# A two-layer encoder on one core: layer 0's V stage at 224 dense tokens instead of 240, layer 1's at 192 instead of 208, two more groups of 16 tokens by table and gather, and six dot products moved to the second half of the U stage

## The chip, the cores and the metric

The kernel runs on one core of a Trainium2 chip. The time is that of the device, in microseconds (us): the median of the runs shown. A profile is one further execution, with its own time. PE is the matrix engine, PEld its weight loads, DVE the vector engine, ACT the scalar engine, POOL the general engine (GpSimd), SP the engine that issues most DMAs here.

## The reference

272 tokens (16 learned ones and 256 of the input) of 1024 numbers go through two layers. Each has a token mixer (layer 0 a gated recurrence in both directions, layer 1 a convolution module), then an expert mixer; each of the four ends in a layer norm over a scaled residual. Nearly all the time is in the two expert mixers:

```python
q = (xc @ w_query).reshape(c, PEER_HEADS, 2, PEER_HALF)
scores = jnp.einsum('chpk,pnk->chpn', q, sub_keys.astype(q.dtype))
s1, i1 = lax.top_k(scores[:, :, 0], PEER_TOPK)
s2, i2 = lax.top_k(scores[:, :, 1], PEER_TOPK)
...
expert = idx1 * PEER_N_KEYS + idx2
g = jax.nn.softmax(s.astype(jnp.float32), axis=-1).astype(xc.dtype)
u = expert_u[expert]
act = jax.nn.gelu(jnp.einsum('chkd,cd->chk', u, xc))
v = expert_v[expert]
return jnp.einsum('chk,chkd->cd', g * act, v)
```

Each token and each of 8 heads picks 16 of 128 x 128 = 16384 experts. An expert has a row of U and a row of V, of 1024 floats each. Layer 1's output for the 16 learned tokens is dropped, so its expert mixer has 256 tokens.

## The kernel before

An expert mixer has two ways to treat a token. The **dense** way multiplies the token with all 16384 rows of U and weighs the results with a matrix that is zero but at the picked experts; then it multiplies the weighed results with all rows of V. The **few** way takes 16 tokens by 8 heads as 128 partitions and, for each of the 16 picks, gathers 128 rows (512 KB) from memory by an indirect DMA that POOL issues (`few_rows`). For U, DVE takes the dot product of the rows with the tokens (`few_mult`, from `few_dot` or from the plan); for V, DVE adds the rows with their weights into `few_out` (`few_add`), and at the end PE adds `few_out` to the accumulators with 8 products by a 0/1 matrix (L770).

A group of 16 tokens is named by its first token. The tables at the top of the file say which way each takes. Tokens below `DENSE_U[layer]` are dense in U, those below `DENSE_V[layer]` dense in V. A group in `EARLY` has its first dots during the first half of U, one in `LATE` has all its dots in the V stage. A group in `DRAWN` is dense in U but few in V: the results of its 16 tokens for all experts are written to a table in memory (`few_dump`: POOL copies a piece to the tile `own` and writes it out), and its 16 activations are then fetched with small indirect DMAs (`few_draw`, L1032; DVE first copies one column of indices to `turn`, L1031).

A layer's mixer is staged so:

- Queries and the top-k. The top-k of the second 128 tokens runs on DVE step by step beside the U stage. Its picks for the groups go through memory (`few_spread`, L994, and `few_fetch`, L998, on POOL), and DVE makes row numbers of them (`few_ids`, L1004 to L1008).
- U, first half: 64 tiles j of 128 experts. Each is one load of 512 KB by SP (`raw`, four buffers), a rounded copy on ACT (`hi`, three buffers), the rest `lo = raw - hi` (L152, two buffers), and 24 products of 128x128 by 240 tokens on PE (L180): hi by the tokens' hi and lo parts, lo by their hi part. `lo` is made by POOL up to tile 40 and by DVE from tile 41.
- U, second half: 64 tiles more, `lo` on DVE. Between them the weight matrix is made and multiplied in, for 8 dense-in-V tokens at a time (`g_unit`: 16 small products on PE, L682 and L683, and some comparisons and products on DVE). `few_dump` writes its pieces here.
- V: 128 tiles. Each is again a load, a `hi`, a `lo` on DVE, and 16 products: hi by the weighed results' hi and lo parts side by side (L732, twice the dense tokens wide) and lo by their hi part (L736, once). The split of the weighed results into parts (`w`) is made for four tiles at once. `few_plan` spreads the gathers of the few groups over tiles 2 to 112 at equal distances: step s issues gather s and then uses gather s - 2; there are three buffers `rows`. It puts the draws of a drawn group between a first tile and three tiles ahead of the group's first V row. Eight tiles before the end SP loads the saved residual `xr` (two DMAs of 512 KB, L759).

The order on each engine is made by a scheduler when the program is built; an engine runs its list in order, and an instruction that waits holds up all behind it. `issue_after(x)` ties what is traced inside it to come after x only where both are on x's engine.

Of the kernel before, what the change touches and what calls it, by code (L numbers as in the profile page):

```python
# [7 lines left out]
F32 = mybir.dt.float32  # L8
F32R = mybir.dt.float32r
F16 = mybir.dt.float16  # L10
U32 = mybir.dt.uint32
# [6 lines left out]
P = 128  # L18
# [6 lines left out]
TOPK = 16  # L25
# [8 lines left out]
FEW = META  # L34
DENSE_U, DENSE_V = (240, 240), (240, 208)
EARLY, LATE, DRAWN = ((256,), (240,)), ((240,), ()), ((), (224, 208))
DOTS_FROM, DOTS, AHEAD, LO_FROM = 48, 10, 2, 41
# [25 lines left out]
class Trunk:  # L63
# [66 lines left out]
    def load(self, src):  # L130
        raw = self.wp.tile([P, NB * P], F32, tag="raw", name="raw", bufs=4)
        parts = src if isinstance(src, tuple) else (src,)
        w = NB * P // len(parts)
        for i, part in enumerate(parts):
            self.nc.sync.dma_start(raw[:, i * w:(i + 1) * w], part)
        return raw
# [408 lines left out]
    def peer(self, layer, n, xs):  # L545
# [10 lines left out]
        with tc.tile_pool(name=f"few{layer}", bufs=1) as kp:  # L556
# [82 lines left out]
            with tc.tile_pool(name=f"act1{layer}", bufs=1) as ap1:  # L639
# [3 lines left out]
                drawn_pool = tc.tile_pool(name=f"drawn{layer}", bufs=2, side="right")  # L643
                rp = drawn_pool.__enter__()
                dumps = {}
                for g, few in enumerate(drawn):
# [47 lines left out]
                def u_out(i, ps):  # L694
# [4 lines left out]
                    if cd > 0:  # L699
                        tmp = hp.tile([P, n], F32, tag="tmp", name="tmp")  # L700
                        nc.scalar.activation(tmp[:, :cd], ps[:, :cd], AF.Gelu_apprx_tanh)
                        nc.vector.tensor_tensor(w[:, :cd], w[:, :cd], tmp[:, :cd], op=OP.mult)  # L702
                    for piece in dumps.get(i, ()):
                        few_dump(*piece)
# [5 lines left out]
                def few_dump(few, j, j1):  # L710
                    own = rp.tile([P, 32, FEW], F32, tag="own", name="own")[:, :j1 - j]
                    act, o = (act_a, 0) if j < JA else (act_b, JA)
                    nc.gpsimd.tensor_copy(own, act[:, j - o:j1 - o, few["t0"]:few["t0"] + FEW])  # L713
                    nc.gpsimd.dma_start(few["table"][:, j:j1], own)
# [33 lines left out]
                for j in range(0, NK - JG, JG):  # L748
# [5 lines left out]
                    if j == NK - 2 * JG:  # L754
                        row_pool.__exit__(None, None, None)
                        self.left_pool = tc.tile_pool(name=f"left{layer}", bufs=1, side="right")
                        xr = self.left_pool.__enter__().tile([P, NB, nq], F32, name="xr")
                        for i in range(2):
                            nc.sync.dma_start(xr[:, 4 * i:4 * i + 4, :], self.saved[:, 4 * i:4 * i + 4, :])  # L759
                    for jj in range(JG):  # L760
# [189 lines left out]
    def few_new(self, kp, layer, t0):  # L950
        few = {"t0": t0, "layer": layer, "rows": {}, "drawn": t0 in DRAWN[layer],
               "ids": kp.tile([P, 2, TOPK], U32, name=f"ids{t0}"), "act": kp.tile([P, TOPK], F32, name=f"act{t0}"),
               "z": kp.tile([P, 1, TOPK], F32, name=f"z{t0}")}
        if t0 < 2 * P:
            few["pos"] = kp.tile([P, 2, TOPK], F32, name=f"pos{t0}")
# [102 lines left out]
    def few_plan(self, vp, early, late, drawn, scale, layer, ahead=2):  # L1058
        tables = self.a["u_rows"], self.a["peer_v"].rearrange("l a b d -> (l a b) d")
        rows = [(few, i, k) for few in early + late + drawn for i in range(2)  # L1060
                for k in range((DOTS if few in early else TOPK if few["drawn"] else 0) if i == 0 else 0, TOPK)]
        begin = 2
        slots = len(rows) + ahead
        at = [begin + s * (NK - 4 * JG - begin) // slots for s in range(slots)]

        def step(s):
            if s >= ahead:
                few, i, k = rows[s - ahead]
                if i == 0:
                    self.few_mult(few, k)  # L1070
                    if k == TOPK - 1:
                        self.few_gelu(few, few is (early + late)[-1])
                else:
# [12 lines left out]
        for g, few in enumerate(drawn):  # L1086
            few["turn"] = vp.tile([P, TOPK], U32, name=f"turn{few['t0']}")
            lo, hi = begin + 14 * g, at[rows.index((few, 1, 0)) + ahead] - 3
            self.steps += [(lo + k * (hi - lo) // TOPK, lambda few=few, k=k: self.few_draw(few, k)) for k in range(TOPK)]
# [254 lines left out]
```

## Time and profile before

| | |
|---|---|
| median of 3 runs | 1810.55 us (1809.45 to 1811.69) |
| the profiled execution | 1811.96 us, span 1810.2 us |
| PE busy | 1760.8 us, 97% of the span |
| DVE busy | 1503.9 us, 83% |
| ACT busy | 908.9 us, 50% |
| POOL busy | 483.8 us, 27% |
| moved from and to memory | 396.41 MB, mean 219 GB/s |
| first half of U, layer 0 and layer 1 | about 125 to 352 and 1047 to 1269 us |
| second half of U | about 352 to 553 and 1270 to 1466 us |
| V | about 553 to 889 and 1466 to 1794 us |

The layers' expert mixers fill 125 to 889 us and 1047 to 1794 us of the span. A row of the timeline gives a start, a duration, engine and line, operation, tiles and count, and in brackets the idle time of the engine before it and what ended it. A row of the chain of waits gives start and duration of a piece of the chain that ended last. A row of the windows gives for one stretch the busy time of PE, PEld, DVE, ACT and POOL with their instruction counts, the clock that PE was granted (1.00 is full speed), the mean busy share of the DMA engines and the rate.

### The profile page before, as it was taken

To read this page: it belongs to the slowest core of one execution; us is meant where nothing else is said; L and a number is where in the kernel's file an instruction comes from. 1 tells how busy PE (TensorE), PEld (TensorE's weight loads), DVE (VectorE), ACT (ScalarE), POOL (GpSimd) and SP (SyncE) were. 2 spreads that over 40 slices of the span, in tenths; PEclk is the share of its full clock that TensorE was granted. 3 is DMA by queue.
4 is the path that set the end of the run, shared out by engine and by line. 5 is a ranking of instruction groups with operands and counts; after the bars stand their busy time and mean duration, and the time that the engine had idled before them with its cause. 6 is when DMAs were issued, how large, how long until landed. Compare 5 with 4: busy or idle time off the path is not lost.

```text
span 1810.2 us, 34904 instructions
## 1 busy us (share of the span) xinstructions
PE 1760.8 (97%) x13484; PEld 1685.9 (93%) x13484; DVE 1503.9 (83%) x2727; ACT 908.9 (50%) x1492; POOL 483.8 (27%) x328
## 2 busy tenths in 40 slices
PE   8999999999999999999998999999999999999996
PEld 7899999999999999999887899999999999999996
DVE  7786998889997777787699769998889968878875
ACT  5554444554445444885432645445454445544452
POOL 1102993100002332221000017962100035634210
PEclk9999999999999999999999999999999999999998
DMA  5446667755557888887541356578555568989973
GB/s 198 163 152 161 195 195 248 253 164 165 169 171 280 307 306 289 293 305 251 192 133 65 105 175 182 182 240 279 186 173 184 172 247 324 329 310 316 321 259 120
DMA packets 112439, 396.41 MB, mean 219 GB/s; under 512 B 13584, under 2 KB 14992, under 8 KB 112144
## 3 DMA queue, kind: packets, MB, share of 16 engines
q1 hardware_dynamic: 91632, 324.74, 53.7%
q0 software_dynamic: 20640, 69.43, 10.8%
q8 instruction: 106, 1.74, 0.4%
q14 instruction: 61, 0.50, 0.1%
HBM read 387.14 MB, written 6.98 MB: 218 GB/s over the span
## 4 chain that ended last, share of the span: by engine, by line
PE 82%; DVE 9%; DMA 3%; POOL 2%; issue 2%; ACT 1%; POOLq 0%; DVEq 0%; SPq 0%; ACTq 0%
PE u L180 40%; PE acc L732 21%; PE acc L736 12%; PE u L216 3%; DVE cy L1224 2%; POOL lo L152 2%; DVE odd L1224 2%; PE g L682 1%; PE g L683 1%; DVE lo L152 1%; DMA raw<-peer_v 1%; DMA rows<-u_rows,ids 1%; PE sps L578 1%; PE var L856 0%; PE acc L770 0%
## 5 line engine op out<-in xcount | busy, mean ns | idle before, releaser
L145 ACT ACTIVATE hi<-raw 128x1024 fp32r<-128x1024 f32 x556 | 588.6, 1059 | 625.3 <-PE u L180 190.9
L152 DVE TENSOR_TENSOR lo<-raw,hi 128x1024 fp32r<-128x1024 f32 x474 | 579.9, 1226 | 173.6 <-PE acc L736 74.7
L180 PE MATMUL u<-xs,hi 128*128 128x240 f32 (+2 forms) x4544 | 569.1, 277 | 0.6 <-DVE xs L379 0.6
L180 PEld LDWEIGHTS u<-xs,hi 128*128 128x128 f32 x4544 | 537.5, 189 | 1.5 <-DVE xs L379 1.2
L732 PE MATMUL acc<-w,hi 128*128 128x480 f32 (+1 forms) x1984 | 448.0, 368 | 4.8 <-ACT hi L145 2.9
L732 PEld LDWEIGHTS acc<-w,hi 128*128 128x128 f32 x1984 | 355.1, 189 | 29.2 <-ACT hi L145 3.2
L180 PE MATMUL u<-xs,lo 128*128 128x240 f32 (+2 forms) x2272 | 308.2, 277 | 5.4 <-POOL lo L152 3.2
L180 PEld LDWEIGHTS u<-xs,lo 128*128 128x128 f32 x2272 | 280.5, 189 | 7.5 <-POOL lo L152 4.2
L736 PEld LDWEIGHTS acc<-w,lo 128*128 128x128 f32 x2048 | 269.4, 191 | 13.5 <-DVE lo L152 5.8
L736 PE MATMUL acc<-w,lo 128*128 128x240 f32 (+1 forms) x2048 | 272.1, 274 | 4.4 <-DVE lo L152 4.4
L152 POOL TENSOR_TENSOR lo<-raw,hi 128x1024 fp32r<-128x1024 f32 x82 | 209.8, 2580 | 100.6 <-ACT hi L145 73.0
L1015 POOL DMA_INDIRECT rows<-peer_v,ids x80 | 122.3, 1529 | 237.6 <-DVE few_out L1056 171.6
L1015 POOL DMA_INDIRECT rows<-u_rows,ids x48 | 59.9, 1249 | 379.2 <-DVE act_b L702 216.0
L216 PE MATMUL u<-x,raw 128*128 128x272 f32 x480 | 114.7, 399 | 5.3 <-DMA x<-h 5.3
L216 PEld LDWEIGHTS u<-x,raw 128*128 128x128 f32 x480 | 92.9, 194 | 24.8 <-DMA raw<-w_in 5.2
L1056 DVE SCALAR_TENSOR_TENSOR few_out<-rows,act,few_out 128x1024 f32<-128x1024 f32 x75 | 96.0, 1280 | 0.0
L689 ACT ACTIVATE act_b<-g 128x432 f32<-128x432 f32 (+41 forms) x56 | 21.9, 390 | 108.8 <-DVE act_b L652 97.4
L665 DVE TENSOR_TENSOR AB<-iota,iT 128x2048 f16<-128x2048 f16 x56 | 68.1, 1219 | 0.1
L1022 DVE SCALAR_TENSOR_TENSOR rows<-rows,wide 128x1024 f32<-128x1024 f32 x48 | 58.5, 1219 | 4.2 <-DMA rows<-u_rows,ids 4.2
L682 PE MATMUL g<-AB 128*128 128x128 f16 x448 | 56.6, 220 | 0.0
L683 PE MATMUL g<-Bl,AB 128*128 128x128 f16 x448 | 56.0, 219 | 0.0
L713 POOL COPY own<-act_b 128x512 f32<-128x512 f32 (+2 forms) x6 | 5.4, 935 | 182.1 <-ACT act_b L698 182.1
(284 smaller groups left out, 1778.6 us busy)
## 6 DMA issues: line engine op xcount, KB each, us to landing
raw<-peer_u SPq DMA_DIRECT2D x256, 512.0 KB, 4.2
raw<-peer_v SPq DMA_DIRECT2D x248, 512.0 KB, 5.1
raw<-w_query SPq DMA_DIRECT2D x28, 512.0 KB, 4.0
raw<-pw SPq DMA_DIRECT2D x22, 512.0 KB, 3.5
raw<-w_in SPq DMA_DIRECT2D x16, 512.0 KB, 4.1
raw<-w_out SPq DMA_DIRECT2D x8, 512.0 KB, 3.9
raw<-peer_v SPq DMA_DIRECT2D x16, 256.0 KB, 4.5
wide<-wide SPq DMA_DIRECT2D x5, 512.0 KB, 4.3
```

What stands on the lines that cost most here:

```text
L145: self.act_hi = nc.scalar.activation(hi, raw, AF.Copy).ins
L152: i = e.tensor_tensor(lo[:, s], raw[:, s], hi[:, s].bitcast(F32), op=OP.subtract)
L180: self.mm = nc.tensor.matmul(ps[:, :n], l[:, k, :], xs(k, r)[:, :n], start=start, stop=stop)
L216: self.mm = self.nc.tensor.matmul(ps[:, :n], raw[:, k, :], x[:, k, :n], start=k == 0, stop=k == NB - 1)
L665: nc.vector.tensor_tensor(AB.rearrange("p x c (a b) -> p (x c) a b", b=2), keys, iT[:, c0 // HC].rearrange("p x c b -> p (x c) b")[:, :, N ...
L682: nc.tensor.matmul(ps[:, c, :], A, Bh, start=True, stop=False)
L683: nc.tensor.matmul(ps[:, c, :], A, Bl, start=False, stop=True)
L732: self.mm = nc.tensor.matmul(acc[b][:, :2 * n].rearrange("p (a t) -> p a t", a=2), hi, w[:, :, :n], start=j == 0, stop=j == NK - JG - 1, s ...
L736: self.mm = nc.tensor.matmul(main[b][:, :n], hi if p_ else lo, w[:, i, :n], start=False, stop=j == NK - 1 and not p_, skip_group_check=True)
L1015: self.nc.gpsimd.indirect_dma_start(out=t, out_offset=None, in_=table, in_offset=bass.IndirectOffsetOnAxis(ap=few["ids"][:, i, k:k + 1], a ...
L1056: nc.vector.scalar_tensor_tensor(few["out"], t, w, few["out"], op0=OP.mult, op1=OP.add)
L1224: nc.vector.scalar_tensor_tensor(z, h, w, z, op0=OP.mult, op1=OP.add)
```

## The change

`DENSE_V` goes from (240, 208) to (224, 192). Layer 0's tokens 224 to 239 and layer 1's tokens 192 to 207 become drawn groups. The last six dots of the early group leave the V stage: they are done in the second half of U, one gather every four tiles into a buffer of its own, and the tokens (`kept`) are loaded once more for them, at the second half's start. `own` has one buffer instead of two. `turn` moves to the pool that lives through the whole mixer, and the draws begin at tile 6 + 12g of V instead of 2 + 14g, g counting a layer's drawn groups. The loads of `xr` are tied behind the last load traced before them.

```diff
-DENSE_U, DENSE_V = (240, 240), (240, 208)
-EARLY, LATE, DRAWN = ((256,), (240,)), ((240,), ()), ((), (224, 208))
+DENSE_U, DENSE_V = (240, 240), (224, 192)
+EARLY, LATE, DRAWN = ((256,), (240,)), ((240,), ()), ((224,), (224, 208, 192))
@@ load
-            self.nc.sync.dma_start(raw[:, i * w:(i + 1) * w], part)
+            self.last_load = self.nc.sync.dma_start(raw[:, i * w:(i + 1) * w], part).ins
@@ peer, ahead of the second half of U
                 rp = drawn_pool.__enter__()
+                self.few_load(rp, early[0], "kept", 1)
@@ u_out, after each tile i of the second half
+                    k, step = divmod(i - 2 + 4 * DOTS, 4)
+                    if step == 0 and DOTS <= k < TOPK:
+                        with tc.issue_after(self.dve_lo.ins):
+                            early[0]["rows"][k] = self.few_rows(rp, early[0], a["u_rows"], 0, k, 1)
+                    if step == 2 and DOTS <= k < TOPK:
+                        with tc.issue_after(self.dve_lo.ins):
+                            self.few_mult(early[0], k)
+                        if k == TOPK - 1:
+                            nc.scalar.activation(early[0]["act"], early[0]["act"], AF.Gelu_apprx_tanh)
@@ few_dump
-                    own = rp.tile([P, 32, FEW], F32, tag="own", name="own")[:, :j1 - j]
+                    own = rp.tile([P, 32, FEW], F32, tag="own", name="own", bufs=1)[:, :j1 - j]
@@ peer, V stage, eight tiles before the end
-                        for i in range(2):
-                            nc.sync.dma_start(xr[:, 4 * i:4 * i + 4, :], self.saved[:, 4 * i:4 * i + 4, :])
+                        with tc.issue_after(self.last_load):
+                            for i in range(2):
+                                nc.sync.dma_start(xr[:, 4 * i:4 * i + 4, :], self.saved[:, 4 * i:4 * i + 4, :])
@@ few_new
+        if few["drawn"]:
+            few["turn"] = kp.tile([P, TOPK], U32, name=f"turn{t0}")
@@ few_plan
-                for k in range((DOTS if few in early else TOPK if few["drawn"] else 0) if i == 0 else 0, TOPK)]
+                for k in range(0 if i or few in late else TOPK, TOPK)]
...
+            if s == ahead and not late:
+                self.warm(AF.Abs_reciprocal_sqrt)
...
-                        self.few_gelu(few, few is (early + late)[-1])
+                        self.few_gelu(few, few is late[-1])
...
-            few["turn"] = vp.tile([P, TOPK], U32, name=f"turn{few['t0']}")
-            lo, hi = begin + 14 * g, at[rows.index((few, 1, 0)) + ahead] - 3
+            lo, hi = 6 + 12 * g, at[rows.index((few, 1, 0)) + ahead] - 3
```

With lines added, the second program's numbers run up to 14 higher: the gathers of L1015 stand at L1028, the copies and writes of L713 and L714 at L723 and L724, the draws of L1032 at L1045.

Three places show what the scheduler made of it. The first is POOL's list in the first half of U of layer 1, from the fetch of the picks on (`pos`), which stands three `lo` after they were written out; in the program before the rows are:

```order
L998 DMA pos_12428<-pos_240_12429 128x32
L998 DMA pos_12434<-pos_224_12435 128x32
L998 DMA pos_12440<-pos_208_12441 128x32
L152 TENSOR_TENSOR lo<-raw,hi 128x1024 x9
L713 COPY own<-act_a 128x512
L714 DMA own_224_15000<-own 128x512
L152 TENSOR_TENSOR lo<-raw,hi 128x1024 x7
L1015 DMA rows<-u_rows,ids_12425 128x1024 x8
```

After the change the same stretch is:

```order
L1011 DMA pos_12500<-pos_240_12501 128x32
L1011 DMA pos_12507<-pos_224_12508 128x32
L1011 DMA pos_12514<-pos_208_12515 128x32
L1011 DMA pos_12521<-pos_192_12522 128x32
L1028 DMA rows<-u_rows,ids_12497 128x1024
L152 TENSOR_TENSOR lo<-raw,hi 128x1024 x9
L723 COPY own<-act_a 128x512
L724 DMA own_224_15091<-own 128x512
L152 TENSOR_TENSOR lo<-raw,hi 128x1024 x7
L1028 DMA rows<-u_rows,ids_12497 128x1024 x8
```

One fetch more, for the fourth group; and a gather of U rows by the picks of group 240 (the first of the six moved dots) now stands ahead of the 16 `lo` that POOL has left to make. The indices that it needs (`ids`) are made by DVE, whose rows for them stand, before and after, behind the whole top-k of the second 128 tokens.

The second place is POOL's list where U ends and V begins in layer 1. Before:

```order
L713 COPY own<-act_b 128x128 x2
L714 DMA own_224_15000<-own 128x128
L714 DMA own_208_15001<-own 128x128
L1015 DMA rows<-u_rows,ids_12425 128x1024 x2
L1032 DMA act_12432<-own_224_15000,turn_17927 128x1
```

After:

```order
L723 COPY own<-act_b 128x128
L724 DMA own_224_15091<-own 128x128
L723 COPY own<-act_b 128x128
L724 DMA own_208_15092<-own 128x128
L723 COPY own<-act_b 128x128
L724 DMA own_192_15093<-own 128x128
L1028 DMA rows<-peer_v,ids_12497 128x1024 x4
L1045 DMA act_12504<-own_224_15091,turn_12506 128x1
```

Three pieces through one buffer, so that each copy waits for the write before it; the first gather of V's plan stands behind them, and its buffer lies on the memory of `own`, so that it waits for the third write. On DVE the first use of that gather, the first row of `few_out`, stands behind the `lo` of V's tile 5 and ahead of that of tile 6:

```order
L264 TENSOR_TENSOR w<-act_a,w 128x4x192
L152 TENSOR_TENSOR lo<-raw,hi 128x1024 x4
L1060 SCALAR_TENSOR_TENSOR act_12498<-act_12498,z_12499 128x16
L264 TENSOR_TENSOR w<-act_a,w 128x4x192
L1067 TENSOR_SCALAR few_out<-rows,act_12498 128x1024
L152 TENSOR_TENSOR lo<-raw,hi 128x1024
```

The third place is SP's list through layer 1's V stage. Before, with the loads of the tokens (`wide`) at its start and of `xr` in its middle:

```order
L135 DMA raw<-peer_v 128x1024 x6
L1043 DMA wide<-wide_240_12651 128x1024
L135 DMA raw<-peer_v 128x1024 x56
L759 DMA xr<-saved_11873 128x1024 x2
L135 DMA raw<-peer_v 128x1024 x62
L135 DMA raw<-peer_v 128x512 x4
```

After, without `wide` there and with `xr` ahead of the last four whole tiles:

```order
L135 DMA raw<-peer_v 128x1024 x120
L770 DMA xr<-saved_11945 128x1024 x2
L135 DMA raw<-peer_v 128x1024 x4
L135 DMA raw<-peer_v 128x512 x4
```

## The prediction

> **What bounds the kernel now.** I read the page first, then the chain of waits, then the windows of the stages that the change touches, then the timeline at the places where PE sits idle.
>
> ```profile
> span 1810.2 us, 34904 instructions
> PE 1760.8 (97%) x13484; PEld 1685.9 (93%) x13484; DVE 1503.9 (83%) x2727; ACT 908.9 (50%) x1492; POOL 483.8 (27%) x328
> PE 82%; DVE 9%; DMA 3%; POOL 2%; issue 2%; ACT 1%; POOLq 0%; DVEq 0%; SPq 0%; ACTq 0%
> ```
>
> PE holds 82% of the chain: products cost time, and the rest counts only where it stops PE. The windows say how much room the others have (columns: PE, PEld, DVE, ACT and POOL busy, granted clock, DMA share, GB/s).
>
> ```profile
> 8.00:20.00 12.00, 12.00 (x48) 9.63 (x48) 10.09 (x44) 2.76 (x7) 0.40 (x2) 1.00 1.02 406
> 355.00:551.00 196.00, 196.00 (x1973) 195.03 (x1973) 179.84 (x269) 95.17 (x212) 0.00 (x0) 1.00 0.54 170
> 553.00:860.00 307.00, 307.00 (x1870) 279.25 (x1871) 235.95 (x229) 184.59 (x275) 79.01 (x54) 1.00 0.83 293
> 1520.00:1621.00 101.00, 101.00 (x680) 100.58 (x679) 83.71 (x93) 49.88 (x50) 56.40 (x42) 1.00 0.91 331
> ```
>
> In the second half of U (second row) transfers run at 170 GB/s, and PE is busy all the time. In V (third row layer 0, fourth layer 1) PE is also always busy, but layer 1 moves 331 GB/s at a DMA share of 0.91; the most seen anywhere is 406 (first row). So V has PE as its bound and transfers close behind.
>
> **Narrower products.** The chain shows tiles of V as a piece of 8 wide products (L732) and one of 8 narrow ones (L736); of layer 0 first, then of layer 1, then an addition of `few_out` (L770) and two rounds of U with a one-hot product between them.
>
> ```profile
> 471.42 5.43 PE u L180 x48
> ...
> 477.76 5.44 PE u L180 x48
> ...
> 624.58 1.76 PE acc L732 x8
> ...
> 629.86 1.76 PE acc L732 x8
> ...
> 1595.89 1.71 PE acc L770 x16
> ...
> 1687.33 1.53 PE acc L732 x8
> ...
> 1696.94 1.15 PE acc L732 x6
> ```
>
> At 240 tokens two tiles take 629.86 - 624.58 = 5.28 us, 2.640 each; at 208 four tiles take 1696.94 - 1687.33 = 9.61, 2.4025 each. Thus 16 tokens are worth 0.1188 us a tile. Each layer loses 16 tokens: 2 x 124 whole tiles x 0.1188 = **-29.5**. Two more drawn groups bring two more additions of 1.71: **+3.4**. The weight matrix is made for 8 tokens at a time, so four units fall away; a unit costs PE 477.76 - 471.42 - 5.43 = 0.91: **-3.6**. The six moved dots cost PE nothing in the second half of U as long as DVE hides there: a dot takes 1.23 us on DVE (the L1022 row where V begins, below), six are 7.4, and 179.8 + 7.4 of 196 still leaves DVE under PE even if I credit nothing for the two units that DVE loses too. Without that cover they would cost their excess, at most some 7 us a layer; I take 0. The same dots leave V, where gathers are what presses.
>
> **The load of `xr`.** In layer 1 PE stops once in mid-V, right after SP's `xr` loads got ahead of tile loads.
>
> ```profile
> 1610.82 0.80 SPq L759 DMA_DIRECT2D xr<-saved  x2
> ...
> 1619.13 1.68 PE L732 MATMUL acc<-w,hi 128*128 128x416 f32 x8
> ...
> 1622.60 1.06 ACT L145 ACTIVATE hi<-raw 128x1024 fp32r<-128x1024 f32 x1 [7.62 <-DMA raw<-peer_v]
> 1623.71 1.90 PE L732 MATMUL acc<-w,hi 128*128 128x416 f32 x8 [2.03 <-ACT hi L145]
> 1626.70 2.04 PE L736 MATMUL acc<-w,lo 128*128 128x208 f32 x8 [1.08 <-DVE lo L152]
> 1632.57 1.69 PE L732 MATMUL acc<-w,hi 128*128 128x416 f32 x8
> ```
>
> ```profile
> 1625.00:1632.00 7.00, 5.92 (x23) 5.31 (x22) 6.31 (x6) 3.42 (x4) 2.10 (x2) 0.52 0.52 180
> ```
>
> ACT waits 7.62 us for a tile, PE idles 2.03 + 1.08, and then runs at a granted clock of 0.52 for some 6.6 us. From 1619.13 to 1632.57 three tiles pass in 13.44 us instead of 3 x 2.4025 = 7.21: a loss of 6.2, of which 3.1 is idle and 3.1 the low clock. After the change `xr` stands ahead of the last four whole tiles, where no gathers are left and 0.52 MB a tile is far under the rates above: **-6.2**, and at least 0 if the 1 MB stops PE there in the same way.
>
> **POOL's list in the first half of U, layer 1.** Here a wait is added. The first moved gather needs DVE's `ids` for group 240 and now stands on POOL ahead of 16 `lo`; PE needs a `lo` for each tile and has two buffers.
>
> ```profile
> 1158.09 16.23 DVE L890 TENSOR_TENSOR cand<-sv 128x2048 f32<-128x2048 f32 x1
> 1158.66 1.68 POOL L998 DMA_DIRECT2D pos<-pos  x3
> 1160.36 23.27 POOL L152 TENSOR_TENSOR lo<-raw,hi 128x1024 fp32r<-128x1024 f32 x9
> 1162.80 1.16 PE L180 MATMUL u<-xs,lo 128*128 128x240 f32 x8 [0.40 <-POOL lo L152]
> 1174.35 0.76 DVE L898 MAX8 fv<-cand 128x8 f32<-128x256 f32 x2
> 1190.38 6.60 DVE L1007 TENSOR_SCALAR ids<-pos 128x16 uint32<-128x16 f32 x2
> 1196.95 2.48 DVE L1008 TENSOR_TENSOR ids<-ids,pos 128x16 uint32<-128x16 uint32 x2
> 1202.30 1.04 POOL L1015 DMA_INDIRECT rows<-u_rows,ids  x1 [0.16 <-DVE ids L1007]
> ```
>
> ```profile
> 261.67 4.20 DVE L890 TENSOR_TENSOR cand<-sv 128x2048 f32<-128x2048 f32 x1
> 281.94 0.93 DVE L1007 TENSOR_SCALAR ids<-pos 128x16 uint32<-128x16 f32 x2
> ```
>
> Before, POOL starts its next `lo` at 1160.36, and PE takes it at 1162.80, already 0.40 late. After, POOL stops behind the fourth fetch. What DVE has left: `cand`, which took 16.23 us while POOL's `lo` ran back to back, but 4.20 in layer 0 where POOL paused between them; with POOL halted I take 4.2, so it ends about 1162.3. The rest up to `ids` took 1190.38 - 1174.35 = 16.0 us, and `ids` itself 0.9 and some in layer 0 against 6.6 and more here. So the indices stand at about 1179, the gather's issue takes 1.04, a `lo` 23.27 / 9 = 2.6: 1182.5 instead of 1162.8, or some **20 us of idle PE**. Then comes the low clock, by the `xr` place 6.6 us at half speed, 3.3 lost: **+23.3**. Bounds: 18 if `cand` is quicker and the clock costs little; about 43 if DVE gains nothing and ends at 1196.95 + 2.48 = 1199.4 as it does now (1199.4 + 1.04 + 2.5 - 1162.8 + 3.3); nothing if the hold were hidden, which two `lo` buffers (5 us) can't do. I stay near the lower end, since the layer 0 rows have DVE beside a pausing POOL. In layer 0 no gather stands ahead of a `lo`; one spread and fetch more on POOL, 1.2 us, is taken as **+0.5**.
>
> **Where V begins, layer 1.** Three pieces go through one `own`, and the first gather of V stands behind the third write.
>
> ```profile
> 1467.00 1.71 POOL L713 COPY own<-act_b 128x128 f32<-128x128 f32 x2 [22.61 <-ACT act_b L698]
> 1468.65 1.06 POOL L714 DMA_DIRECT2D own<-own  x2
> 1473.15 0.15 DVE L1031 COPY turn<-ids 128x1 uint32<-128x1 uint32 x1 [2.14 <-DMA own<-own]
> 1473.47 1.92 POOL L1015 DMA_INDIRECT rows<-u_rows,ids  x1 [3.75 <-DVE turn L1031]
> ...
> 1481.67 1.23 DVE L1022 SCALAR_TENSOR_TENSOR rows<-rows,wide 128x1024 f32<-128x1024 f32 x1 [3.97 <-DMA rows<-u_rows,ids]
> 1482.04 1.78 PE L732 MATMUL acc<-w,hi 128*128 128x416 f32 x8 [0.84 <-ACT hi L145]
> ...
> 1485.04 1.15 PE L736 MATMUL acc<-w,lo 128*128 128x208 f32 x8 [1.22 <-DVE lo L152]
> ```
>
> ```profile
> L1054 DVE TENSOR_SCALAR few_out<-rows,act x5: 747/750/754, 599.2 to 1670.2; 128x1024 f32<-128x1024 f32 x5
> ...
> DMA to landing us min/median/max: 4.2/6.8/10.3
> ```
>
> (The last two rows are of the tile `rows`: its first use in ns, and the landing of its gathers.) A piece is a copy of 0.86 and a write that lands about 3.9 later (1469.2 to 1473.15): three are 14.3, from 1467.0 to 1481.3. The gather lands 6.8 later, 1488.1; the first row of `few_out` (0.75) and the `lo` of tile 6 (1.2) bring 1490. PE wants that `lo` at 1485.04 - 1.22 - 0.84 - 7 x 0.12 = 1482.1: idle 7.9, and 3.3 for the clock, less the 2.06 that PE idles here now: **+9.1**. Bounds: 3 (landing at 4.2, no clock loss) and 17 (each write 2.6 later). In layer 0 there is one piece, and its gather lands in time: 0.
>
> **Transfers in V, layer 1.** Gathers go from one per 1.964 tiles (54 and 2 steps over 110 tiles) to one per 1.667 (64 and 2): 0.524 + 0.524/1.667 = 0.839 MB a tile. PE's pace would be 2.4025 - 0.119 = 2.285 us, which asks for 367 GB/s. The nearest rows: 331 with PE never idle, 406 at the most. At 331 a tile takes 2.535, so the cost lies between 0 and 0.25 x 110 = 27. I take a tile of 2.36 us (355 GB/s, a third of the way from 331 to 406), since 0.91 of DMA share at 331 leaves some room: 0.075 x 110 = **+8.3**. Layer 0 asks 0.839/2.52 = 333 GB/s, which layer 1 shows to be held: 0. By the Trainium skill (DMA: Bandwidth & Descriptors, Specifications) the limit per core is about 358 GB/s; its estimate is 2.34 us a tile, +6.3, and the sum 2 lower. The 406 of the first window does not bear that limit out.
>
> **Sum.** -29.5 + 3.4 - 3.6 - 6.2 + 23.3 + 0.5 + 9.1 + 8.3 = +5.3. The profiled execution took 1811.96, 1.4 over the median of 1810.55. So 1817.3 for a profile and **1816** for the median.
>
> **Rivals.** 0.2% (3.6 us) is about what a measurement here can tell from no change.
> 1. *The hold on POOL costs nothing*, because DVE's indices are there when POOL arrives. Then 1816 - 23.3 = 1793, faster. For it: DVE is the engine that POOL's `lo` slow down. Against: 16 us of top-k stand behind `cand` whatever POOL does. It decides once DVE ends by 1163.
> 2. *V keeps PE's pace*: 1816 - 8.3 = 1808, and 1799 with the stop at V's start covered too. For it: 406 GB/s. Against: ACT's waits in mid-V are already for `raw`.
> 3. *Transfers hold V at 331 GB/s*: + 27.5 - 8.3 = 1835. For it: the share of 0.91. Against: PE never idles at that rate, so it was not a limit.
> 4. *The clock comes back sooner.* If half clock lasted half as long, both clock terms would be 1.7: 1813, no change. Against it stands the 6.6 us of the `xr` place. By the Trainium skill (TensorE: Matmul & The Clock Gate, What's actually happening) the rate halves after an idle window of about 3.4 us and is back after 3.4 us of work; by that an idle of 2 us would be free, and the trace, where 2.03 us was followed by 0.52, does not agree.
>
> **How the numbers follow.** The forecast 0.47, with a range of its own of 1806 to 1825; rivals 0.12, 0.18, 0.16 and 0.07. Rival 1 and the upper half of rival 3 (0.08) are left out of the range: **1799 to 1831**. Faster: rival 1, over half of rival 2, a little of the forecast's low end, 0.26. Same: rival 4, the rest of rival 2, some of the forecast, 0.22. Slower: 0.52.
>
> **What would show it.** In the profile after: in layer 1's first half of U one idle of PE of some 20 us ended by POOL's `lo`, with POOL's gather waiting for DVE `ids`; about 8 us of idle PE near tile 6 of its V; no stop around `xr`; tiles of 2.52 us in layer 0's V and 2.36 in layer 1's, at about 355 GB/s. An idle in U under 10 us, or tiles of layer 1 at 2.29, make the prediction wrong downwards; tiles above 2.45, or an idle above 30, upwards.

## The result, and the profile after

The changed kernel takes 1826.28 us (median of 4 runs, 1824.0 to 1829.45), the kernel before 1810.74 (4 runs, 1809.45 to 1811.69). The ratio is 1.0087, with a 95% interval of 1.007 to 1.0103: slower by 15.5 us. The forecast was 1816, slower. The profiled execution took 1825.04 us, 13.1 more than that of before. The head of its page and its chain of waits:

```profile
span 1823.3 us, 35063 instructions
PE 1742.3 (96%) x13452; PEld 1683.1 (92%) x13452; DVE 1515.4 (83%) x2780; ACT 902.1 (49%) x1491; POOL 605.0 (33%) x420
PE 72%; DVE 17%; DMA 4%; issue 3%; ACT 2%; POOL 1%; POOLq 0%; DVEq 0%; SPq 0%; ACTq 0%
```

PE has 18.5 us less to do, and the span is 13.1 us longer. Its share of the chain falls from 82% to 72%, and DVE's rises from 9% to 17%. So PE waits, and the question is where. Each stage is measured from its first product on PE to that of the next (us):

| stage | before | after | difference | forecast |
|---|---|---|---|---|
| layer 0, U | 433.3 | 440.6 | +7.3 | -1.3 |
| layer 0, V | 338.0 | 323.4 | -14.6 | -13.0 |
| between the mixers | 150.8 | 150.5 | -0.3 | 0 |
| layer 1, U | 424.7 | 448.2 | +23.5 | +21.5 |
| layer 1, V and the end | 343.7 | 341.3 | -2.4 | -1.8 |

(The forecast by stage is made of the prediction's terms, the units of the weight matrix counted in U and the additions in V. The start of the span gives the missing -0.4.) One stage is far off, the first.

**Layer 1, U.** The timeline of the changed kernel at the place where POOL's gather now stands ahead of `lo`:

```profile
1151.09 3.65 DVE L901 TENSOR_TENSOR cand<-sv 128x2048 f32<-128x2048 f32 x1
1152.51 2.22 POOL L1011 DMA_DIRECT2D pos<-pos  x4
...
1170.80 0.23 DVE L1020 TENSOR_SCALAR ids<-pos 128x16 uint32<-128x16 f32 x2
1171.45 1.04 POOL L1028 DMA_INDIRECT rows<-u_rows,ids  x1 [16.72 <-DVE ids L1017]
...
1172.50 7.09 POOL L152 TENSOR_TENSOR lo<-raw,hi 128x1024 fp32r<-128x1024 f32 x3
1174.92 2.06 PE L180 MATMUL u<-xs,lo 128*128 128x240 f32 x8 [18.65 <-POOL lo L152]
1176.78 3.48 PE L180 MATMUL u<-xs,hi 128*128 128x240 f32 x16
1180.09 1.06 PE L180 MATMUL u<-xs,lo 128*128 128x240 f32 x8
```

POOL stands 16.72 us in front of the gather, and PE idles 18.65 us for the next `lo`. `cand` took 3.65 us instead of 16.23. It ended at 1154.74, together with the issue of POOL's four fetches, so it had hardly any of the halt to run in; the first experiment below shows that it is as short without the halt. The eight and sixteen products after the idle take 1180.09 - 1174.92 = 5.17 us instead of 2.69 (the same pieces before run at 0.90 and 1.79): 2.5 us for the low clock, which the window from 1172 to 1178 has at 0.50 (third figure from the end):

```profile
1172.00:1178.00 6.00, 3.08 (x14) 3.08 (x15) 6.00 (x3) 1.43 (x2) 5.97 (x4) 0.50 0.55 175
```

**Layer 0, U.** Here the forecast saw nothing of size. Before, at the same place:

```profile
231.43 0.86 POOL L994 DMA_DIRECT2D pos<-idx  x1
232.26 5.11 DVE L924 TENSOR_TENSOR oh<-oh,s 128x512 f16<-128x512 f16 x1
...
283.07 1.23 DVE L152 TENSOR_TENSOR lo<-raw,hi 128x1024 fp32r<-128x1024 f32 x1
...
285.70 1.23 DVE L152 TENSOR_TENSOR lo<-raw,hi 128x1024 fp32r<-128x1024 f32 x1 [0.46 <-PE u L180]
```

After:

```profile
231.08 1.47 POOL L1007 DMA_DIRECT2D pos<-idx  x2
231.91 18.57 DVE L935 TENSOR_TENSOR oh<-oh,s 128x512 f16<-128x512 f16 x1
232.56 7.10 POOL L152 TENSOR_TENSOR lo<-raw,hi 128x1024 fp32r<-128x1024 f32 x3
239.60 1.14 POOL L1011 DMA_DIRECT2D pos<-pos  x2
240.76 11.98 POOL L152 TENSOR_TENSOR lo<-raw,hi 128x1024 fp32r<-128x1024 f32 x5
...
292.35 0.23 DVE L1020 TENSOR_SCALAR ids<-pos 128x16 uint32<-128x16 f32 x2
...
293.24 1.22 DVE L152 TENSOR_TENSOR lo<-raw,hi 128x1024 fp32r<-128x1024 f32 x1
294.51 2.06 PE L180 MATMUL u<-xs,lo 128*128 128x240 f32 x8 [7.58 <-DVE lo L152]
```

One small product of DVE, which ended between two `lo` of POOL after 5.11 us, now takes 18.57: seven `lo` and the issue of two fetches on POOL pass before it ends. All of DVE's list behind it moves back, its first `lo` (tile 41) from 283.07 to 293.24. Before, DVE was ahead there by a little (its second `lo` already waits 0.46 us for PE); after, PE waits 7.58 us, with 2.4 more at the low clock (294.51 to 299.58, 5.07 us for pieces that take 2.69).

**V.** A piece of the chain in layer 0's V, wide and narrow products in turn, and a stretch of PE's timeline in layer 1's:

```profile
602.74 1.62 PE acc L742 x8
604.35 0.88 PE acc L746 x8
...
607.74 1.62 PE acc L742 x8
```

```profile
1522.38 1.65 PE L742 MATMUL acc<-w,hi 128*128 128x384 f32 x8
...
1527.05 1.65 PE L742 MATMUL acc<-w,hi 128*128 128x384 f32 x8
```

Layer 0 at 224 tokens: (607.74 - 602.74) / 2 = 2.50 us a tile. Layer 1 at 192: (1527.05 - 1522.38) / 2 = 2.333, for two neighbouring tiles without a wait, not the forecast 2.285. The windows of layer 1's V, and ACT's waits for a load between 1510 and 1780 (us in all, how often, the longest):

```profile
1510.00:1600.00 90.00, 87.77 (x593) 86.61 (x592) 77.32 (x97) 44.09 (x46) 61.48 (x51) 0.98 0.92 332
1600.00:1700.00 100.00, 98.32 (x674) 96.52 (x673) 85.54 (x93) 50.38 (x52) 61.16 (x41) 1.00 0.93 340
```

```profile
ACT hi L145 <- DMA raw<-peer_v: 101.2, 71, 4.4
```

PE is no longer always busy: it idles 2.2 of 90 and 1.7 of 100 us. Tiles 10 to 120, additions included, take 272.7 us, where 110 x 2.333 + 4 x 1.71 would be 263.5; 9.2 us are lost in small waits. At V's start the three pieces go one by one:

```profile
1482.43 0.44 POOL L723 COPY own<-act_b 128x128 f32<-128x128 f32 x1 [13.12 <-ACT act_b L699]
1485.18 1.19 POOL L723 COPY own<-act_b 128x128 f32<-128x128 f32 x1 [1.48 <-DMA own<-own]
1490.54 0.29 POOL L723 COPY own<-act_b 128x128 f32<-128x128 f32 x1 [3.34 <-DMA own<-own]
...
1496.15 1.00 POOL L1028 DMA_INDIRECT rows<-peer_v,ids  x1 [4.48 <-PE acc L746]
...
1501.00 0.75 DVE L1067 TENSOR_SCALAR few_out<-rows,act 128x1024 f32<-128x1024 f32 x1 [7.25 <-DMA rows<-peer_v,ids]
...
1502.94 2.02 PE L746 MATMUL acc<-w,lo 128*128 128x192 f32 x8 [5.33 <-DVE turn L1044]
```

The gather starts 5.02 us after the third write is issued at 1491.13. The idle of 5.33 us ends with DVE's `lo` behind the first use of the gather (the row names `turn`, a copy that ends just before this `lo`); the low clock behind it costs some 2.2 us. Around the `xr` loads PE stops no more.

### The profile page after: what moved, and what is told of

It reads as the page before. It is cut to its first block, busy times and chain, and to the rows that moved or that the text cites. A ratio compares the mean times of both kernels' runs of the same rounds, so it can differ in the third digit from the quotient of the medians.

```text
span 1823.3 us, 35063 instructions
## 1 busy us (share of the span) xinstructions
PE 1742.3 (96%) x13452; PEld 1683.1 (92%) x13452; DVE 1515.4 (83%) x2780; ACT 902.1 (49%) x1491; POOL 605.0 (33%) x420
## 3 DMA queue, kind: packets, MB, share of 16 engines
q0 software_dynamic: 27200, 88.43, 13.1%
## 4 chain that ended last, share of the span: by engine, by line
PE 72%; DVE 17%; DMA 4%; issue 3%; ACT 2%; POOL 1%; POOLq 0%; DVEq 0%; SPq 0%; ACTq 0%
PE u L180 36%; PE acc L742 18%; PE acc L746 11%; DMA raw<-peer_v 3%; PE u L216 3%; DVE cy L1238 2%; DVE lo L152 2%; DVE odd L1238 2%; PE g L683 1%; PE g L684 1%; DVE oh L935 1%; POOL lo L152 1%; ACT hi L145 1%; PE acc L781 1%; DVE x L363 1%
## 5 line engine op out<-in xcount | busy, mean ns | idle before, releaser
L742 PE MATMUL acc<-w,hi 128*128 128x448 f32 (+1 forms) x1984 | 424.4, 356 | 2.9 <-DVE w L264 1.9
L742 PEld LDWEIGHTS acc<-w,hi 128*128 128x128 f32 x1984 | 350.3, 190 | 13.7 <-DVE w L264 2.2
L746 PEld LDWEIGHTS acc<-w,lo 128*128 128x128 f32 x2048 | 267.1, 192 | 19.2 <-DVE lo L152 14.8
L746 PE MATMUL acc<-w,lo 128*128 128x224 f32 (+1 forms) x2048 | 271.5, 274 | 11.1 <-DVE turn L1044 6.5
L1028 POOL DMA_INDIRECT rows<-peer_v,ids x112 | 184.4, 1646 | 187.1 <-DVE few_out L1069 103.4
L1028 POOL DMA_INDIRECT rows<-u_rows,ids x48 | 66.2, 1378 | 241.2 <-DVE rows L1035 198.3
L1069 DVE SCALAR_TENSOR_TENSOR few_out<-rows,act,few_out 128x1024 f32<-128x1024 f32 x105 | 134.6, 1282 | 5.2 <-DMA rows<-peer_v,ids 5.1
L723 POOL COPY own<-act_b 128x512 f32<-128x512 f32 (+2 forms) x12 | 10.5, 876 | 249.3 <-ACT act_b L699 230.9
L1045 POOL DMA_INDIRECT act<-own,turn x64 | 75.6, 1181 | 22.5 <-issue 17.1
L690 ACT ACTIVATE act_b<-g 128x488 f32<-128x488 f32 (+35 forms) x52 | 20.2, 388 | 103.8 <-DVE act_b L653 89.9
L666 DVE TENSOR_TENSOR AB<-iota,iT 128x2048 f16<-128x2048 f16 x52 | 63.7, 1229 | 0.1
```

The costliest lines, as they stand in the source:

```text
L666: nc.vector.tensor_tensor(AB.rearrange("p x c (a b) -> p (x c) a b", b=2), keys, iT[:, c0 // HC].rearrange("p x c b -> p (x c) b")[:, :, N ...
L742: self.mm = nc.tensor.matmul(acc[b][:, :2 * n].rearrange("p (a t) -> p a t", a=2), hi, w[:, :, :n], start=j == 0, stop=j == NK - JG - 1, s ...
L746: self.mm = nc.tensor.matmul(main[b][:, :n], hi if p_ else lo, w[:, i, :n], start=False, stop=j == NK - 1 and not p_, skip_group_check=True)
L1028: self.nc.gpsimd.indirect_dma_start(out=t, out_offset=None, in_=table, in_offset=bass.IndirectOffsetOnAxis(ap=few["ids"][:, i, k:k + 1], a ...
L1045: self.nc.gpsimd.indirect_dma_start(out=few["act"][:, k:k + 1], out_offset=None, in_=few["table"].rearrange("p j (t o) -> (p j t) o", o=1) ...
L1069: nc.vector.scalar_tensor_tensor(few["out"], t, w, few["out"], op0=OP.mult, op1=OP.add)
```

## The experiments

All times are medians, and each run of a kernel has runs of the kernel before beside it (1809.7 in each of the three groups of runs). The first four kernels ran together.

**The gather behind POOL's last `lo`.** One tie more in the second half of U:

```diff
-                        with tc.issue_after(self.dve_lo.ins):
+                        with tc.issue_after(self.dve_lo.ins), tc.issue_after(self.lo_ins.ins):
                             early[0]["rows"][k] = self.few_rows(rp, early[0], a["u_rows"], 0, k, 1)
```

> The changed kernel, but the first of the six moved gathers is tied behind POOL's last `lo`, so that POOL's list in layer 1's first half of U has no gather ahead of a `lo`. Theory A (the hold costs its own idle time and the low clock behind it): 18.65 us of idle PE and some 3.3 us of clock go, 1826.3 - 22 = 1804. Rival B (what the hold gave DVE is lost again: without POOL's `lo` DVE finished the top-k some 28 us earlier, 1171.6 against 1199.4, and when POOL runs on, DVE is late where it takes over `lo` at tile 41, as it was in layer 0): a new idle of some 8 us with its clock, 1826.3 - 22 + 12 = 1816. Under both, layer 0 keeps its idle of 7.6 us.

Measured: 1803.82 us, ratio 0.9973 (0.996 to 0.9986). In layer 1's U nothing over 1 us is left but the 1.41 us before a POOL `lo` that the kernel before has too; the stage takes 425.3 us instead of 448.2. Rival B falls: DVE does not come late, because the halt had given it next to nothing. POOL's `lo` run on behind the four fetches here, and `cand` is as short as with the halt:

```profile
1153.50 3.63 DVE L901 TENSOR_TENSOR cand<-sv 128x2048 f32<-128x2048 f32 x1
...
1154.91 2.22 POOL L1011 DMA_DIRECT2D pos<-pos  x4
1157.14 14.31 POOL L152 TENSOR_TENSOR lo<-raw,hi 128x1024 fp32r<-128x1024 f32 x6
```

`cand`'s length in layer 1 goes with the number of fetches that POOL issues there: 16.20 to 16.49 us in the five profiles of this case with three, 3.59 to 3.65 in the nine with four. Why is not shown. Layer 0's idle stands as it was:

```profile
230.95 18.93 DVE L935 TENSOR_TENSOR oh<-oh,s 128x512 f16<-128x512 f16 x1
...
293.75 2.06 PE L180 MATMUL u<-xs,lo 128*128 128x240 f32 x8 [7.57 <-DVE lo L152]
```

So the largest single cost of the change is where one gather stands in POOL's list; with it gone, the change is faster than the kernel before by 0.27%.

**Layer 0's `lo` by POOL to tile 44.** On top of that (the diff also lets the steps of the top-k that run beside DVE's `lo` start four tiles later):

```diff
+                lo_from = LO_FROM + 4 * (layer == 0)
...
-                    if j >= LO_FROM and len(picked[-1]) == 2:
+                    if j >= lo_from and len(picked[-1]) == 2:
...
-                ... lambda j: FULL if j >= LO_FROM else (("p", 1024),), u_store)
+                ... lambda j: FULL if j >= lo_from else (("p", 1024),), u_store)
```

> The run with the tied gather, and in layer 0 POOL makes `lo` up to tile 44 instead of 40, the top-k's steps beside U starting four tiles later too. Theory A (layer 0's idle of 7.58 us stands because DVE, starved in one product for 18.57 us, reaches its first `lo` late; four tiles are 10.8 us of room): the idle and its low clock of 3 to 5 us go, 10 to 12 us less than the run with the tied gather alone, 1793. Rival B (the time DVE lacks is moved to tile 45 or to the end of the first half of U, where the dots begin): 0 to 4 us less.

Measured: 1792.88 us, ratio 0.9904 (0.9883 to 0.9924), 10.9 less. The idle at tile 41 is gone and none stands at tile 45; layer 0's U takes 431.7 us instead of 440.6. Theory A holds: what was late is DVE at the takeover. The product itself is still held, for 21.27 us in this profile; the four tiles of room hide it.

**One `own` tile for the last three pieces.** On top of both:

```diff
-                    own = rp.tile([P, 32, FEW], F32, tag="own", name="own", bufs=1)[:, :j1 - j]
+                    if j1 < NK or few is drawn[0]:
+                        dumps["own"] = rp.tile([P, 32, FEW], F32, tag="own", name="own", bufs=1)
+                    o = drawn.index(few) * (j1 - j) if j1 == NK else 0
+                    own = dumps["own"][:, o:o + j1 - j]
```

> The run before it in this list, and the last three pieces of layer 1 go into three parts of one `own` tile, so that no copy waits for the write before it. Theory A (the stop at V's start is the chain of three copies and writes): the third write lands 6 to 8 us earlier, the idle of 5.33 us at tile 6 and its low clock of about 3.3 go, 8 us less. Rival B (the stop is the gather's own way: issue to use was 4.9 us and the buffer is free only once U's memory is): at most 3 us less.

Measured: 1788.88 us, ratio 0.9889 (0.9866 to 0.9912), 4.0 less, between the two (layer 1's V and the end take 335.9 us instead of 339.0 in the profiles). In its timeline the three pieces follow without a wait, and the first gather starts 7.3 us after the first copy (1450.73 to 1458.02) instead of 13.7; the idle is 1.86 us, and no low clock follows:

```profile
1458.02 1.58 POOL L1033 DMA_INDIRECT rows<-peer_v,ids  x1 [3.48 <-PE acc L751]
...
1465.78 0.75 DVE L1072 TENSOR_SCALAR few_out<-rows,act 128x1024 f32<-128x1024 f32 x1 [3.79 <-DMA rows<-peer_v,ids]
...
1467.72 1.14 PE L751 MATMUL acc<-w,lo 128*128 128x192 f32 x8 [1.86 <-DVE turn L1049]
```

The chain of writes was the larger part of the stop (the idle was 4.39 us in the kernel one step before). What is left is the gather's own way to its use, which also became longer: 7.76 us from its issue to the first row of `few_out`, against 4.85 in the change. The 8 us expected counted on the whole stop going.

**`xr` alone, in the kernel before.**

```diff
+                        with tc.issue_after(self.last_load):
                             for i in range(2):
                                 nc.sync.dma_start(xr[:, 4 * i:4 * i + 4, :], self.saved[:, 4 * i:4 * i + 4, :])
```

> The kernel before, with nothing but the `xr` loads tied behind the last load. Theory A (the stop in mid-V is these two loads ahead of tiles): 3.1 us of idle and 3.1 of low clock go, 1810.7 - 6.2 = 1804.5. Rival B (the loads are 1 MB that a stage near the transfers' limit has to carry somewhere): the stop goes but the time shows up at the end, 1808 to 1811.

Measured: 1805.16 us, ratio 0.9976 (0.9965 to 0.9988), 4.5 less. In the profile layer 1's V, from its first wide product to its last, falls from 326.7 to 321.0 us, and no stop stands in its middle or at its end. Theory A holds, with 4.5 to 5.7 us for 6.2.

The next three kernels have the version so far as their base ("the fixed version": late gather, takeover at 45, one `own` tile). They ran together with the one that moves the spread, in a second group of runs.

**Half the gathers in layer 1's V.**

```diff
-                few["rows"][k] = self.few_rows(vp, few, tables[i], i, k, ahead + 1)
+                if layer and k % 2:
+                    few["rows"][k] = few["last"]
+                else:
+                    few["last"] = few["rows"][k] = self.few_rows(vp, few, tables[i], i, k, ahead + 1)
```

> The fixed version (late gather, `lo` of layer 0 by POOL to tile 44, one `own` tile), but in layer 1's V every second gather is left out and its addition takes the rows gathered before it, so the result is not the reference's; DVE's work stays. In the fixed version tiles 0 to 120 of that stage take 298 us; PE's own pace is 120 x 2.333 + 4 x 1.71 = 287. Theory A (transfers hold the stage: ACT waits for `raw`, then DVE's `lo` is late): the 11 us shrink to 3 or less, the time falls by some 8 us to 1781. Rival B (DVE, with 1.28 us of addition every 1.67 tiles beside its `lo`, is what is late): 1787 to 1790.

**Half the additions in layer 1's V.**

```diff
-                    self.few_add(vp, few, k)
+                    if layer and k % 2:
+                        t = few["rows"].pop(k)
+                        self.nc.vector.tensor_copy(few["act"][:, k:k + 1], t[:, :1])
+                    else:
+                        self.few_add(vp, few, k)
```

> The fixed version, with all gathers, but in layer 1's V every second addition to `few_out` is left out (a copy of one column stands in its place), so the result is not the reference's. Theory A (transfers): nothing moves, 1786 to 1790. Rival B (DVE): the waits for `lo` go, some 8 us, 1781.

Measured: 1785.49 us with half the gathers (0.9863, 0.9835 to 0.9891) and 1789.92 with half the additions (0.9889, 0.9861 to 0.9917), against 1788.88 of the fixed version: the times do not tell them apart. Stops elsewhere differ by as much as the few us in question: the idle at V's start, 1.86 us in the fixed version, is 3.55 and 2.98 in these, and in layer 1's U the profile with half the gathers has one idle of 3.03 us with low clock behind it, where the fixed version has 0.61, so that its U is 5.9 us longer while its V and the end are 7.4 us shorter (328.5 against 335.9).

```profile
1258.92 2.06 PE L180 MATMUL u<-xs,lo 128*128 128x240 f32 x8 [3.03 <-DVE lo L152]
```

The windows of one stretch, and ACT's waits for loads in it, do tell. The fixed version, half the gathers, half the additions:

```profile
1490.00:1760.00 270.00, 264.50 (x1823) 259.83 (x1822) 224.93 (x245) 133.65 (x137) 128.73 (x97) 1.00 0.92 331
...
ACT hi L145 <- DMA raw<-peer_v: 110.4, 76, 4.4
```

```profile
1490.00:1760.00 270.00, 269.59 (x1870) 268.99 (x1869) 231.01 (x251) 137.22 (x140) 99.80 (x71) 1.00 0.84 280
...
ACT hi L145 <- DMA raw<-peer_v: 65.4, 49, 3.9
```

```profile
1490.00:1760.00 270.00, 267.58 (x1845) 265.25 (x1844) 195.90 (x246) 135.72 (x137) 126.83 (x99) 1.00 0.94 333
...
ACT hi L145 <- DMA raw<-peer_v: 96.0, 69, 3.3
```

PE idles 5.5 us, 0.4 us and 2.4 us of 270, and tiles 10 to 120 lose 9.1, 0.5 and 4.2 us against PE's pace of 2.333. Fewer gathers take nearly all of PE's waits away with DVE as busy as before, and ACT waits for loads 65.4 us instead of 110.4, so transfers hold the stage, as forecast. (The run takes POOL's issues away along with the transfers; but the waits of the fixed version name no engine that waits for POOL.) Fewer additions take half of PE's waits at the same rate of transfers: a late tile costs PE more when DVE also has an addition ahead of its `lo`. Neither theory alone gives both.

**Two drawn groups in layer 1.**

```diff
-DENSE_U, DENSE_V = (240, 240), (224, 192)
-EARLY, LATE, DRAWN = ((256,), (240,)), ((240,), ()), ((224,), (224, 208, 192))
+DENSE_U, DENSE_V = (240, 240), (224, 208)
+EARLY, LATE, DRAWN = ((256,), (240,)), ((240,), ()), ((224,), (224, 208))
```

> The fixed version with layer 1's V dense for 208 tokens and two drawn groups, as in the kernel before. Theory A (in layer 1 the third group gives PE 124 x 0.069 - 1.7 = 6.9 us and takes about as much in waits for transfers): 1787 to 1792, no difference from three groups. Rival B (the third group's gain stays): 1795 to 1797.

Measured: 1785.15 us, ratio 0.9863 (0.9846 to 0.9879), under both forecasts. To settle the few us between two and three groups, both ran once more in the third group of runs:

> The fixed version with two groups in layer 1, beside the one with three on the same chip. Theory A (the third group's gain for PE of 6.9 us is given back whole in V): within 3 us of the one with three groups. Rival B (it gives back more than it gains): 3 to 6 us under the one with three.

> The fixed version with three groups, beside the one with two on the same chip: 1787 to 1791 under both theories, and the difference decides between them.

Measured: 1786.85 (0.9869, 0.9851 to 0.9887) with two and 1795.33 (0.9923, 0.99 to 0.9946) with three. The version with three is over the 1787 to 1791 that both theories gave it, and some 6 us over its own first median of 1788.88. The kernel with two is the faster by 8.5 us beside it, more than either theory said, and by 3.7 from the first group of runs to the second. Not all of the 8.5 comes from the third group: in the profiles of these two runs layer 0's V, whose tables are the same, is 2.4 us longer with three. In layer 1 alone, U, V and the end are 4.1 us shorter with two groups in the first pair of profiles and 2.3 in the second. With two, PE idles 0.3 us of the same 270, and tiles 10 to 120 lose 0.7 us:

```profile
1490.00:1760.00 270.00, 269.68 (x1818) 268.20 (x1817) 211.78 (x218) 136.71 (x138) 97.48 (x69) 1.00 0.87 302
```

So layer 1's third group gives back more than it gains, by 2 to 4 us in layer 1 itself by these profiles, and the version with two is the fastest here: 1.3 to 1.4% under the kernel before, 2.1 to 2.2% under the change.

**The spread one `lo` later in layer 0.** On the version with the gather tied alone:

```diff
-                    if j == SPREAD:
+                    if j == SPREAD + (layer == 0):
...
-                    if j == SPREAD + 3:
+                    if j == SPREAD + 3 + (layer == 0):
```

> The version with only the gather tied (1803.8, idle of 7.57 us in layer 0 at tile 41), and in layer 0 POOL's spread and fetch of the picks each stand one `lo` later. Theory A (DVE's product that took 18.57 us loses the port at each change of one POOL `lo` to the next, and where POOL's pauses fall decides how long): the product takes another time, between 1 and 12 us, and the idle shrinks by what it gains; at 5 us, the time that it took before the change, the idle and its clock are gone, 1793. Rival B (the second spread and fetch cost POOL and DVE their own 1.2 us each and the rest, wherever they stand): the idle stays at 7 to 9 us, 1803 to 1806.

Measured: 1812.52 us, ratio 1.0019 (1.0006 to 1.0031), 8.7 us more than its base in the first group of runs. The timeline:

```profile
232.57 2.34 DVE L935 TENSOR_TENSOR oh<-oh,s 128x512 f16<-128x512 f16 x1
...
234.58 1.47 POOL L1007 DMA_DIRECT2D pos<-idx  x2
235.90 20.30 DVE L1020 TENSOR_SCALAR ids<-idx 128x16 uint32<-128x16 f32 x2
...
297.85 2.06 PE L180 MATMUL u<-xs,lo 128*128 128x240 f32 x8 [10.26 <-DVE lo L152]
```

Half of theory A holds: the product now takes 2.34 us. But the hold went to another instruction, which again stands at POOL's writes of the picks: the first of the two in the row took 20.22 us, and the idle grew to 10.26. Rival B, a fixed cost, gave 7 to 9 us of idle and 1803 to 1806, and falls.

**The dots back in V**, in the version with two groups: the second half of U without its gathers and dots, and the plan with the last six dots of the early group, as in the kernel before.

```diff
-                for k in range(0 if i or few in late else TOPK, TOPK)]
+                for k in range((DOTS if few in early else TOPK if few["drawn"] else 0) if i == 0 else 0, TOPK)]
```

> The fixed version with two drawn groups in layer 1 (1785.2), and the six dots put back into V, as in the kernel before; no gather stands in U beyond the first ten. Theory A (the dots cost nothing in the second half of U and their gathers crowd V only where transfers are at their limit): layer 0 has 70 gathers over 110 tiles (one every 1.53 tiles at 2.50 us), 0.867 MB a tile or 346 GB/s, and loses some 3 us; layer 1 is as the kernel before with the `xr` tie, and pays its stop of 2 to 3 us at V's start and low clock again: 1788 to 1793. Rival B (moving the dots was worth nothing): 1783 to 1787.

Measured: 1787.85 us, ratio 0.9877 (0.9859 to 0.9895), 1.0 over the 1786.85 beside it: no difference that this can tell. In the profile layer 0's V is 4.7 us longer (341.5 against 336.8) with single stops up to 1.3 us, but layer 1's U is 2.5 us shorter and its V 0.7 longer (317.8 and 317.1). That moving the dots is worth anything by itself is not shown.

**The change again**, in the same group of runs:

> The change itself, on the same chip as its fixed versions. If the two holds in U are settled by the program and not by chance in a run, the idle of 18 to 19 us in layer 1 and of 7 to 8 us in layer 0 stand again, and the time is 1824 to 1829.

Measured: 1824.87 us, ratio 1.0077 (1.005 to 1.0103). Its idles are 18.66 us in layer 1, as expected, and 10.27 in layer 0, more than the 7 to 8 expected; there the starved product took 21.26 us: the holds are the program's, but the length of the second changes from run to run, here by about one `lo` of POOL.

## Why the prediction was right, and where it was not

The sign and the range hold: 1826.28 lies within 1799 to 1831, in the case with 0.52. The likeliest figure, 1816, is 10 us low, and one term of the sum is that far off: layer 0's U. Without its 10.9 us the change would stand at 1815.4; that this is so near 1816 is in part luck, since the products gave 3.9 us less than forecast and V's start cost 3.6 less.

- **POOL's list in layer 1 (+23.3)**: the hold is right in mechanism and size. 18.65 us of idle against 20; 2.5 us of low clock against 3.3; 21 to 23 us by the run that takes it away. One premise came true in another way than it was argued: the prediction took a short `cand` because POOL would be halted, and `cand` is as short (3.63 us) where POOL runs on. No run has a halt behind three fetches, so what the halt alone would have done is not shown. Rival 1, that the hold costs nothing, is out.
- **Layer 0's U (+0.5)**: the step that failed. The prediction said of layer 0 that no gather stands ahead of a `lo` and priced the second spread and fetch at POOL's own 1.2 us. What stands in its place is a product of DVE that POOL's `lo` hold up, and it costs 10.0 us by the profile (7.58 and 2.4), 10.9 by the run that gives DVE room for it. That the second write is what prolongs the product is read from the profiles (one write: 5.11 us, and 2.34 in the run of `xr` alone; two: 18.57 to 21.28 in eleven); no run changes that alone. The prediction had used the other side of this effect, DVE's 16.23 us for `cand` beside POOL's `lo`, and did not ask what happens to DVE where POOL's pauses move. It also did not read how little DVE was ahead at tile 41: 0.46 us of waiting for PE in the row of its second `lo`. With 10.0 in place of 0.5 the sum is +14.8; measured are +13.1 by the profile and +15.5 by the medians.
- **Narrower products (-29.5)**: mis-sized by carrying one slope on. The pace is 2.640, 2.503, 2.4025 and 2.333 us a tile at 240, 224, 208 and 192 tokens, so 16 tokens are worth 0.137, 0.101 and 0.070. Layer 0 gets 17.0, layer 1 8.6, together 25.6. The narrow products take 0.88 to 0.89 us at 240, 224 and 208 alike, a row that the prediction did not use. (Over eight tiles in a row without a wait, in the run with half the gathers, the mean at 192 is 2.325; with it layer 1 gets 9.5, and the waits below are 0.9 larger.)
- **`few_out` (+3.4), units (-3.6), dots (0)**: within what the stages show; layer 0's V, forecast at -13.0, gave -14.6.
- **`xr` (-6.2)**: right, 4.5 to 5.7 by its own run.
- **V's start (+9.1)**: right in mechanism, too large: 5.33 + 2.2 - 2.06 = 5.5. The gather's rows were used 4.85 us after its issue, against 6.8 for the landing; the three pieces took 13.7 us against 14.3; and the low clock cost 2.2 and not 3.3.
- **Transfers in layer 1's V (+8.3)**: right in size and cause: 9.2 us of waits, of which the run with half the gathers leaves 0.5 of 9.1. But it stands on a pace of 2.333, not 2.285, so tiles 10 to 120 average 2.42 us with the additions taken out, and not 2.36. Rival 2 (PE's pace is kept) and rival 3 (331 GB/s for all, 2.535) are both out; 350 GB/s is reached for 80 us in the fixed version at a DMA share of 0.97.
- **The clock (rival 4)**: half clock cost 2.5, 2.4 and 2.2 us after idles of 18.65, 7.58 and 5.33, between the 3.3 used and the rival's 1.7. The prediction's own rows around `xr` have this size too: from 1626.70 to 1632.57, 5.87 us for pieces that take 3.3, a loss of 2.6. By the Trainium skill (TensorE: Matmul & The Clock Gate, What's actually happening), at least one busy window of about 3.4 us brings the rate back, an estimated loss of 1.7 us or more; here PE ran 5.1 to 5.4 us for pieces that take 2.7 to 3.2, so the losses lie above that estimate.

In layer 1's V three misses largely cancelled: PE's pace gave 6.1 us less than forecast, V's start cost 3.6 less, the waits 0.9 less against before (9.2 less the 1.8 that stood there besides `xr`). These three and the rest of the stage leave some 2 us that no row here accounts for.

## What to carry to other kernels

An instruction that is tied to another engine's work only is free on its own: look in the built order at what it now stands ahead of, since one early gather cost here more than 16 tokens saved in a layer. Where one engine's instructions are starved by another's, a DMA more on the second can move the delay, either way: with one write more a product took 13 us longer in layer 0, and with one fetch more `cand` took 13 us less in layer 1. So price such a change by how little the first engine is ahead where it is next needed, not by the DMA's own time. And a width's price per token should be read between the two widths nearest to the new one: here the slope from 240 to 208 overstated the gain from 208 to 192.

## What was not expected of the hardware

DVE instructions that stood at POOL's DMA issues, with back-to-back `lo` of POOL behind these, took long here: 18.57 to 21.28 us for one product of 128x512 (in the eleven profiles in which POOL issues two writes there), 20.22 for a tensor by scalar operation of 128x16, and 16.20 to 16.49 for `cand` where POOL issues three fetches. The same product took 5.11 us before, at a single write of POOL, and 2.34 where it waited for a single `lo`; `cand` took 3.59 to 3.65 where POOL issued four fetches behind its `lo`. The long ones end when POOL pauses or goes from one `lo` to the next; the issue of two fetches in the midst (239.60 to 240.74 in the change) did not end one. By the Trainium skill (SBUF — State Buffer, Who interferes with whom), a product of DVE with two inputs and a reading instruction of POOL can't run at once, and the second to start is blocked until the first finishes; the 2.34 us agree with that, but the 18 to 21 us span several `lo`, each of 2.4 us, so here the one that waits did not get the next turn. The tensor by scalar operation reads one tile and not two, so what is said here of two inputs does not cover its 20.22 us. What decides at which of these DVE gets its turn is open; no run here isolates it.
